# First attention, heads 4 to 7: probabilities turned by VectorE blocks and one exchange through HBM instead of TensorE, with the values one unit later and the branch product behind retention's projections

## The chip, the cores and the metric

The kernel runs on one core of one Trainium2 chip. The metric is device time in microseconds (us). The kernel before took 815.37 us, the median of three runs (815.24 to 815.68). A difference under 0.2% (1.6 us) can't be told from no change.

The engines are named as in the profile: PE (TensorE), DVE (VectorE), ACT (ScalarE), POOL (GpSimd) and SP (SyncE, which here only issues DMAs). Each engine runs its own instructions in order and waits on semaphores that other engines or DMAs raise.

## The reference, cut to what matters

Two layers, each a mixer and a squared-ReLU MLP, on 256 tokens of width 1024. The mixer adds three branches: MLA attention (called the first attention here), MoBA attention, and retention with a group norm.

```python
def causal_attention(q, k, v, scale):            # MLA: 8 heads
    s = einsum('bhqd,bhkd->bhqk', qb, k) * scale  # 128 queries at a time
    p = softmax(where(kpos <= qpos, s, NEG_INF))
    return einsum('bhqk,bhkd->bhqd', p, v)

def hybrid_mixer(h, w_in, ...):
    p = h @ w_in     # all projections: cq, ckv, k_rope, mq, mk, mv, rq, rk, rv, rg, g_mla, g_moba, g_ret
    o_mla, o_moba, o_ret = mla_branch(...), moba_branch(...), retention_branch(...)
    merged = (sigmoid(g_mla) * (o_mla @ w_branch_mla)
              + sigmoid(g_moba) * (o_moba @ w_branch_moba)
              + sigmoid(g_ret) * (o_ret @ w_branch_ret))
    return merged @ w_out
```

With 256 tokens MoBA has a single block, so it is causal attention too. Everything is float32; the kernel keeps that precision by splitting each large operand into a high and a low part and multiplying three times.

## The kernel before, in words

**Units.** The mixer is a list `prog` of units. A unit is a piece of a weight product on PE: in `project` and `branch` one weight block of 128x1024 numbers (512 KB) and 12 matmuls of 512 columns; in `project_turned` one block, 8 matmuls of 512 columns and 8 of 256. `at(slot, job)` hangs other work behind a unit. The order of the units of a layer, before: start or `b0` and `mq`, `mk`, `mv` with `qrope`, `qnope`, `kvup`; the gates `gmla0`, `gmla1`, `gmoba0`, `gmoba1` (4 units each); `bmla0`, `bmla1` (2 each, the first attention's branch product); `rqk` (4 units, retention's queries and keys); `rv`, `rg`, `gret0`, `gret1` (4 each); `bmoba0`, `bmoba1`, `bret0`, `bret1` (2 each); `wout`; then the MLP. Within this order a list scheduler places the instructions of each engine before the program runs, by its own estimate of times. PE's order is fixed by it, and so are DVE's, ACT's and SP's.

**A weight block's way.** SP issues the DMA into a `raw` tile (7 of them), ACT copies it to `whi` (L222), DVE subtracts to `wlo` (L224), PE uses both. `behind` names DMAs after which a weight block is to be issued.

**Attention.** Scores go to four PSUM banks (`ps_s`); DVE adds the mask and takes the maximum, ACT does exp, DVE the reciprocal and the scaling (L538). The values product `po` (L609, L611) needs the probabilities turned, keys along partitions. There are two ways to turn them. `turned_blocks` transposes 32x32 blocks on DVE (a STREAM_TRANSPOSE per head into a tile `blocks`), and `moved_blocks` (L594) moves the blocks to their partitions with 16 DMAs from SBUF to SBUF. `turned` transposes on PE, three 128x128 matmuls against the identity per head into a PSUM bank `ps_pt` (L549), which ACT copies out (L550). The first attention's heads 0 to 3 go the first way, its heads 4 to 7 the second (`homes` = `("probT", None)`), in both layers. MoBA's eight heads go the first way.

**What hangs where.** `first` is the unit at which an attention's scores of heads 0 to 3 start: `mv` 3 for the first attention, `gmoba1` 1 for MoBA. Just ahead of MoBA's first scores stand the first attention's values (`former`). `ret_scores` (`ps_r`) stands behind MoBA's values at `rg` 1. `ret_values` (`por`, L1042 to L1044), `group_norm` and `oret_blocks` hang at `rg` 3.

**Retention's way to its branch.** After `por`: `group_norm` on DVE, POOL and ACT; `oret_blocks` transposes blocks on DVE (L273), one DMA of 512 KB writes them to a `bounce` in HBM (L275) and four of 128 KB read them back turned (`oretturned`, L279); `oret_split` copies them to `oreth` on ACT and to `oretl` on DVE (L264); then PE can start `bret0`. The MLP turns its hidden rows the same way (`hblocks`, `hturned`).

**Rope.** `swapped` (L464) makes the partner halves `qkoth` of queries or keys with four SBUF-to-SBUF DMAs; products with sine and cosine follow (L476). For MoBA in the first layer POOL does them, eight such DMAs for heads 0 to 3 and eight for heads 4 to 7; for retention in both layers DVE does most of it.

Of the kernel before, what the change touches and what calls it, by code (L numbers as in the profile page):

```python
# [7 lines left out]
F32 = mybir.dt.float32  # L8
F32R = mybir.dt.float32r
BF16 = mybir.dt.bfloat16  # L10
AF = mybir.ActivationFunctionType
# [3 lines left out]
P = 128  # L15
D = 1024
S = 256
# [15 lines left out]
QKD = NOPE + ROPE  # L33
# [29 lines left out]
def weight_plan():  # L63

    plan = []

    def block(key, name, kt, cols, per):
        for j in range(0, kt, per):
            plan.append(((*key, j // per), name, (j, per), cols))

    def turned(key, cols):
        for n in range(4):
            block((*key, n), "w_in", KD, cols[P * n : P * n + P], KD)

    def span(c, n):
        return range(c, c + n)

    for l in range(L):
        if l == 0:

            for i in range(2):
                plan.append(((l, "mq", i), "w_in", (0, 1), C_MQ[256 * i : 256 * i + 256]))
            plan.append(((l, "b0", 0), "w_in", (0, 1), C_MLA))
            for k in range(1, KD):
                plan.append(((l, "b0mq", k), "w_in", (k, 1), [*C_MLA, *C_MQ]))
        else:
            block((l, "b0"), "w_in", KD, C_MLA, 2)
            turned((l, "mq"), C_MQ)
        turned((l, "mk"), C_MK)
        block((l, "mv"), "w_in", KD, C_MV, 2)  # L90
        mv, plan = plan[-4:], plan[:-4]
        for i, (key, name, kt, cols) in enumerate(
            (("qrope", "mla_w_q_up", 2, C_QROPE), ("qnope", "mla_w_q_up", 2, C_QNOPE), ("kvup", "mla_w_kv_up", 1, C_KV))
        ):
            block((l, key), name, kt, cols, kt)
            plan.append(mv[i])
        plan.append(mv[3])
        for i in range(2):
            block((l, "gmla%d" % i), "w_in", KD, span(C_GMLA + 512 * i, 512), 2)
        for i in range(2):  # L100
            block((l, "gmoba%d" % i), "w_in", KD, span(C_GMOBA + 512 * i, 512), 2)
        def branch_block(name, i):
            block((l, "b%s%d" % (name, i)), "w_branch_" + name, 4, span(512 * i, 512), 2)

        for i in range(2):
            branch_block("mla", i)
        turned((l, "rqk"), C_RQK)
        block((l, "rv"), "w_in", KD, C_RV, 2)
        block((l, "rg"), "w_in", KD, span(C_RG, 512), 2)
        for i in range(2):  # L110
            block((l, "gret%d" % i), "w_in", KD, span(C_GRET + 512 * i, 512), 2)
        for name, i in LATE:
            branch_block(name, i)
        for n in range(KD):
            block((l, "wout", n), "w_out", KD, span(P * n, P), KD)
        for kind, i in mlp_order():
            if kind == "up":
                g, j = divmod(i, 4)
                plan.append(((l, "up", g, j), "w_mlp_up", (2 * j, 2), span(512 * g, 512)))
            else:  # L120
                plan.append(((l, "down", i, 0), "w_mlp_down", (i, 1), range(D)))
    at, offset = {}, 0
    for key, name, (j, n), cols in plan:
        at[key] = (offset, n, len(cols))
        offset += P * n * len(cols)
    return plan, at, offset
# [22 lines left out]
def trunk(ctx: ExitStack, tc: tile.TileContext, gx, wts, consts, gfin, gn, xtok, out):  # L149


    nc = tc.nc
# [34 lines left out]
        return loaded.pop(key)  # L187


    behind = {}  # L190

    def have(n):

# [39 lines left out]
    def misc_tile(name="misc"):  # L233
        return ps.tile([P, 512], F32, name=name, tag="misc", bufs=4)
# [260 lines left out]
    def in_a_row(*jobs):  # L495


        with tc.manual_schedule(engines={mybir.EngineType.PE}):
            rest = [job() for job in jobs]
        for job in rest:  # L500
            job()
# [14 lines left out]
    def attention_head(scale):  # L516


        got = {}

        def scores(s_ps):
            p = sb.tile([P, 3 * P], F32, name="prob", bufs=4)
            m = small("smx")
            nc.vector.tensor_tensor_reduce(
                p[:, 0:P], s_ps[:, 0:P], mask[:, P : 2 * P], 1.0, NEG_INF, ALU.add, ALU.max, m[:, 0:1]
            )
            nc.vector.tensor_tensor_reduce(
                p[:, P : 3 * P], s_ps[:, P : 3 * P], mask, 1.0, NEG_INF, ALU.add, ALU.max, m[:, 1:2]
            )
            nc.vector.tensor_scalar(m[:, 2:4], m[:, 0:2], -scale, None, op0=ALU.mult)  # L530
            spans = ((0, P), (P, 3 * P))
            for i, (a, b) in enumerate(spans):
                nc.scalar.activation(
                    p[:, a:b], p[:, a:b], AF.Exp, bias=m[:, 2 + i : 3 + i], scale=scale, accum_out=m[:, 4 + i : 5 + i]
                )
            nc.vector.reciprocal(m[:, 6:8], m[:, 4:6])
            for i, (a, b) in enumerate(spans):
                nc.vector.tensor_scalar(p[:, a:b], p[:, a:b], m[:, 6 + i : 7 + i], None, op0=ALU.mult)  # L538
            got["p"] = p

        def turn_blocks(dst):

            return nc.vector.transpose(dst, got["p"])

        def turn(dst):

            pt = misc_tile("ps_pt")
            for i, src in enumerate((0, P, 2 * P)):
                nc.tensor.transpose(pt[:, P * i : P * i + P], got["p"][:, src : src + P], ident)  # L549
            return lambda: nc.scalar.activation(dst, pt[:, : 3 * P], AF.Copy)  # L550

        return scores, turn_blocks, turn

    def attention(oT, vs, scale, first, group, former, gap, turn, homes):

# [5 lines left out]
        def four_tile(h):  # L561
            if h // 4 not in tiles:
                tiles[h // 4] = sb.tile([P, 4 * 3 * P], F32, name="probT", bufs=2)
            return tiles[h // 4]
# [12 lines left out]
                tc.keep_in_program_order(turning)  # L577
            pT[h] = o[:, 0:2], o[:, 2]

        def turned(h):  # L580

            o = four_tile(h)[:, 3 * P * (h % 4) : 3 * P * (h % 4) + 3 * P]
            pT[h] = o[:, 0:S], o[:, S : 3 * P]
            return heads[h][2](o)

        def moved_blocks(h0):


            e = 3 * P
            for a in range(4):  # L590
                for b in range(4):
                    src = pT["blocks"][32 * a : 32 * a + 32, e * b : e * b + e]
                    queue = nc.scalar if h0 and b % 2 else nc.sync
                    dma = queue.dma_start(four_tile(h0)[32 * b : 32 * b + 32, e * a : e * a + e], src)  # L594
                    if former:
                        tc.keep_in_program_order(dma)

# [29 lines left out]
        at(first, lambda: in_a_row(*former, lambda: four(0)))  # L627
        at(first + gap, lambda: in_a_row(lambda: four(4)))
        for i in range(2):
            if homes[i] is None:  # L630
                at(first + turn[i], lambda i=i: in_a_row(*(lambda h=h: turned(h) for h in range(4 * i, 4 * i + 4))))
                continue
            for h in range(4):
                at(first + turn[i] + h // 2, lambda h=4 * i + h: turned_blocks(h, heads[h][1]))
            at(first + turn[i] + 1, lambda i=i: moved_blocks(4 * i))
# [91 lines left out]
    def at(slot, step):  # L727
        steps.setdefault(slot, []).append(step)

    def slot(key, j):  # L730
        return [k for k, _ in prog].index((key, j))
# [8 lines left out]

    def layer(l, xn, before):

        c0 = []
        c, mla, mqkv, rqkv = {}, {}, {}, {}

# [218 lines left out]
        def mla_scores(h0):  # L964
# [4 lines left out]
            return banks  # L969

        mla_last = attention(
            omlaT, lambda: mla["v"], QKD**-0.5, first, mla_scores, (), MLA_GAP, MLA_TURN, ("probT", None)
        )


# [3 lines left out]
        def load_dec():  # L979

            rqkv["dec"] = sb.tile([P, K_TURNED_MB - K_DEC], F32, name="dec", tag="Q", bufs=1)
            tc.keep_in_program_order(nc.sync.dma_start(rqkv["dec"], consts[:, K_DEC:K_TURNED_MB]))

        at(slot("gmoba1", 3), load_dec)
        merged, mT = {}, []
        branch(l, "bmla", range(2), omlaT, th_mla, merged)
        if l == 0:

            for i, (key, j) in enumerate((("gmoba0", 0), ("gmoba0", 1), ("gmoba1", 0), ("gmoba1", 1))):
                at(slot(key, j), lambda i=i: moba_rope(("mk", "mq")[i % 2], i // 2))  # L990
        first = slot("gmoba1", 1)
        at(first, lambda: omobaT.extend((t4("omobah"), t4("omobal"))))

        def moba_scores(h0):
# [87 lines left out]
                split_turned(oret_T[0], oretT)  # L1082

        project_turned(l, "rqk", xn, ret_pair)
        project(l, "rv", xn, 512, ret_done("rv"))


# [38 lines left out]
        branches = {"moba": (omobaT, th_moba), "ret": (oretT, th_ret)}  # L1126
        for name, half in LATE:
            branch(l, "b" + name, [half], *branches[name], merged, between if name == "ret" else None)
        at(slot("rg", 1), lambda: in_a_row(*moba_last, ret_scores))
        for h in range(RT_H):  # L1130
            at(slot("rg", 3), lambda h=h: ret_values(h))
        at(slot("rg", 3), group_norm)
        at(slot("rg", 3), oret_blocks)
        at(slot("bmoba1", 1), oret_split)


# [238 lines left out]
MLA_GAP = 7  # L1375
# [84 lines left out]
```

## Time and profile before

| | |
|---|---|
| median of three runs | 815.37 us |
| the profiled execution's own time | 816.03 us |
| its span, first to last instruction | 814.1 us |
| PE busy in the span | 807.1 us, 99% |
| DVE busy | 577.3 us, 71% |
| ACT busy | 459.9 us, 56% |
| POOL busy | 98.2 us, 12% |
| granted TensorE clock | 0.999 |
| first attention's values on PE in the first layer start at | 100.8 us |
| retention's branch product in the first layer starts at | 196.0 us |

Times in the views are microseconds from the span's start. Matmuls overlap: one of 512 columns is shown as lasting 0.39 us, while the next one starts 0.23 us after it. What PE spends on a matmul is therefore read from start to start.

### The profile page before, as it was taken

To read this page: it belongs to the slowest core of one execution; us is meant where nothing else is said; L and a number is where in the kernel's file an instruction comes from. 1 tells how busy PE (TensorE), PEld (TensorE's weight loads), DVE (VectorE), ACT (ScalarE), POOL (GpSimd) and SP (SyncE) were. 2 spreads that over 40 slices of the span, in tenths; PEclk is the share of its full clock that TensorE was granted. 3 is DMA by queue.
4 is the path that set the end of the run, shared out by engine and by line. 5 is a ranking of instruction groups with operands and counts; after the bars stand their busy time and mean duration, and the time that the engine had idled before them with its cause. 6 is when DMAs were issued, how large, how long until landed. Compare 5 with 4: busy or idle time off the path is not lost.

```text
span 814.1 us, 11424 instructions
## 1 busy us (share of the span) xinstructions
PE 807.1 (99%) x3991; PEld 677.1 (83%) x3991; DVE 577.3 (71%) x950; ACT 459.9 (56%) x722; POOL 98.2 (12%) x75
## 2 busy tenths in 40 slices
PE   9999999999999999999999999999999999999996
PEld 7888888888888888888899888888888888888885
DVE  6879599798786455555598985886898754665554
ACT  7676655445555455555586565645546645555551
POOL 0100440330030000000035221012201200000000
PEclk9999999999999999999999999999999999999999
DMA  9964665767476777776657539448674676898731
GB/s 334 350 232 133 223 219 190 254 217 271 143 224 214 236 256 259 260 256 236 212 176 218 180 107 367 143 130 282 219 239 162 219 242 227 294 301 282 255 133 52
DMA packets 65528, 182.14 MB, mean 224 GB/s; under 512 B 9024, under 2 KB 23744, under 8 KB 65216
## 3 DMA queue, kind: packets, MB, share of 16 engines
q1 hardware_dynamic: 64128, 179.97, 65.8%
q10 hardware_dynamic: 1344, 1.46, 0.6%
q8 instruction: 31, 0.51, 0.3%
q14 instruction: 25, 0.20, 0.1%
HBM read 161.47 MB, written 11.53 MB: 213 GB/s over the span
## 4 chain that ended last, share of the span: by engine, by line
PE 99%; DVE 0%; ACT 0%; issue 0%; DVEq 0%
PE acc L245 18%; PE acc L243 18%; PE acc L244 18%; PE pup L244 7%; PE pup L243 7%; PE pup L245 7%; PE acc L1150 6%; PE acc L442 5%; PE acc L444 2%; PE ps_s L968 1%; PE acc L810 1%; PE po L609 1%; PE ps_s L511 1%; PE warm L721 0%; PE acc L812 0%; PE po L611 0%
## 5 line engine op out<-in xcount | busy, mean ns | idle before, releaser
L224 DVE TENSOR_TENSOR wlo<-raw,whi 128x1024 fp32r<-128x1024 f32 (+4 forms) x287 | 340.6, 1206 | 107.1 <-ACT whi L222 104.7
L222 ACT ACTIVATE whi<-raw 128x1024 fp32r<-128x1024 f32 (+4 forms) x287 | 287.7, 1022 | 167.7 <-PE acc L245 89.6
L243 PE MATMUL acc<-whi,xs 128*128 128x512 f32 (+1 forms) x304 | 118.5, 391 | 0.0
L245 PE MATMUL acc<-whi,xs 128*128 128x512 f32 (+1 forms) x304 | 118.4, 389 | 0.0
L244 PE MATMUL acc<-wlo,xs 128*128 128x512 f32 (+1 forms) x304 | 117.8, 387 | 0.0
L244 PE MATMUL pup<-wlo,xs 128*128 128x512 f32 x256 | 99.8, 390 | 0.0
L243 PE MATMUL acc<-whi,sq 128*128 128x512 f32 x256 | 99.8, 390 | 0.0
L245 PE MATMUL pup<-whi,xs 128*128 128x512 f32 x256 | 99.6, 389 | 0.0
L245 PE MATMUL acc<-whi,sq 128*128 128x512 f32 x256 | 99.6, 389 | 0.0
L244 PE MATMUL acc<-wlo,sq 128*128 128x512 f32 x256 | 99.6, 389 | 0.0
L243 PE MATMUL pup<-whi,xs 128*128 128x512 f32 x256 | 99.3, 389 | 0.0
L264 DVE TENSOR_TENSOR sq<-hturned,sq 128x1024 fp32r<-128x1024 f32 x16 | 19.6, 1225 | 75.5 <-ACT sq L264 75.5
L243 PEld LDWEIGHTS acc<-whi,xs 128*128 128x128 f32 x304 | 57.0, 188 | 11.5 <-issue 0.7
L245 PEld LDWEIGHTS acc<-whi,xs 128*128 128x128 f32 x304 | 57.1, 188 | 11.4
L244 PEld LDWEIGHTS acc<-wlo,xs 128*128 128x128 f32 x304 | 57.1, 188 | 11.0
L264 ACT ACTIVATE sq<-hturned 128x1024 fp32r<-128x1024 f32 x16 | 17.0, 1060 | 79.6 <-DMA hturned<-bounce 79.6
L243 PEld LDWEIGHTS acc<-whi,sq 128*128 128x128 f32 x256 | 48.1, 188 | 10.0
L245 PEld LDWEIGHTS acc<-whi,sq 128*128 128x128 f32 x256 | 48.1, 188 | 10.0
L244 PEld LDWEIGHTS acc<-wlo,sq 128*128 128x128 f32 x256 | 48.0, 188 | 9.9
L245 PEld LDWEIGHTS pup<-whi,xs 128*128 128x128 f32 x256 | 48.1, 188 | 9.8
L244 PEld LDWEIGHTS pup<-wlo,xs 128*128 128x128 f32 x256 | 48.1, 188 | 9.7
L243 PEld LDWEIGHTS pup<-whi,xs 128*128 128x128 f32 x256 | 47.9, 188 | 9.8
(216 smaller groups left out, 1137.5 us busy)
## 6 DMA issues: line engine op xcount, KB each, us to landing
raw<-wts SPq DMA_DIRECT2D x264, 512.0 KB, 4.6
bounce<-hblocks SPq DMA_DIRECT2D x16, 512.0 KB, 4.7
hturned<-bounce SPq DMA_DIRECT2D x64, 128.0 KB, 2.9
probT<-blocks SPq DMA_DIRECT2D x80, 48.0 KB, 2.0
qkoth<-qkraw SPq DMA_DIRECT2D x48, 64.0 KB, 2.4
raw<-wts SPq DMA_DIRECT2D x5, 464.0 KB, 6.0
dec<-consts SPq DMA_DIRECT2D x2, 1024.0 KB, 6.6
raw<-wts SPq DMA_DIRECT2D x4, 416.0 KB, 4.1
```

The source lines that it names most:

```text
L222: fetched.append(nc.scalar.activation(hi[:, cs], raw[:, cs], AF.Copy))
L224: nc.vector.tensor_sub(lo[:, cs], raw[:, cs], hi[:, cs].bitcast(F32))
L243: nc.tensor.matmul(o, ah, bh, start=start, stop=False, **more)
L244: nc.tensor.matmul(o, ah, bl, start=False, stop=False, **more)
L245: nc.tensor.matmul(o, al, bh, start=False, stop=stop, **more)
L264: return nc.scalar.activation(hi, src, AF.Copy), nc.vector.tensor_sub(lo, src, hi.bitcast(F32))
L442: nc.tensor.matmul(acc, wh[:, k, :], xn.both(k), start=k == 0, stop=False)
L444: nc.tensor.matmul(acc[:, 0:S], wl[:, k, :], xn.k(k)[0], start=False, stop=k == KD - 1)
L511: mm = nc.tensor.matmul(bank[:, o], a[rows, sa], b[rows, sb_], start=True, stop=True)
L609: nc.tensor.matmul(dst, vh, pT[h + j][0], start=True, stop=False)
L810: nc.tensor.matmul(mq[n], wq[n][0], xn.both(k), start=k == 0, stop=False)
L1150: nc.tensor.matmul(o, a, b, start=half == 0 and i == 0, stop=4 * half + n == KD and i == len(jobs) - 1)
```

## The change

The first attention's heads 4 to 7 are turned by DVE blocks as well, into the tile of the keys (`"KK"`, whose readers are done by then). The PE way and its ACT copies are gone from the program. For these four heads `moved_blocks` no longer issues 16 DMAs from SBUF to SBUF: one DMA of 768 KB writes the blocks to `pbounce` in HBM, and four of 192 KB read them back into `probT`, one for each band of 32 partitions.

SP would otherwise be free to issue other DMAs between; `behind` and `issue_after` set two of them after the exchange: the load of retention's decay table `dec` (1 MB), and one weight block (the first layer's fourth `rqk` block, the second layer's second `bmla0` block).

The units are reordered. `rqk` comes right behind `gmoba1`, and `bmla0` and `bmla1` come behind `rqk`. The first attention's values and MoBA's first scores move from `gmoba1` 1 to `gmoba1` 2. MoBA's values and `ret_scores` move from `rg` 1 to `rg` 2, and `ret_values`, `group_norm` and `oret_blocks` from `rg` 3 to `gret0` 0. `oret_split` stays at `bmoba1` 1.

```diff
@@ weight_plan
+        turned((l, "rqk"), C_RQK)
         for i in range(2):
             branch_block("mla", i)
-        turned((l, "rqk"), C_RQK)
@@ attention_head, attention
-        def turn(dst):
-            pt = misc_tile("ps_pt")
-            for i, src in enumerate((0, P, 2 * P)):
-                nc.tensor.transpose(pt[:, P * i : P * i + P], got["p"][:, src : src + P], ident)
-            return lambda: nc.scalar.activation(dst, pt[:, : 3 * P], AF.Copy)
...
         def moved_blocks(h0):
             e = 3 * P
+            tile_ = four_tile(h0)
+            if h0 and not former:
+                bounce = dr.tile([P, 4 * e], F32, name="pbounce", bufs=1)
+                nc.sync.dma_start(bounce, pT["blocks"])
+                for b in range(4):
+                    src = bounce.rearrange("(a p) (b r) -> b p a r", a=4, b=4)[b]
+                    dst = tile_[32 * b : 32 * b + 32].rearrange("p (a r) -> p a r", a=4)
+                    behind[tuple(mla_next)] = [nc.sync.dma_start(dst, src)]
+                return
             for a in range(4):
                 for b in range(4):
...
         for i in range(2):
-            if homes[i] is None:
-                at(first + turn[i], lambda i=i: in_a_row(*(lambda h=h: turned(h) for h in range(4 * i, 4 * i + 4))))
-                continue
             for h in range(4):
                 at(first + turn[i] + h // 2, lambda h=4 * i + h: turned_blocks(h, heads[h][1]))
             at(first + turn[i] + 1, lambda i=i: moved_blocks(4 * i))
@@ layer
+        mla_next[:] = (l, "bmla0", 1) if l else (l, "rqk", 3, 0)
...
-            omlaT, lambda: mla["v"], QKD**-0.5, first, mla_scores, (), MLA_GAP, MLA_TURN, ("probT", None)
+            omlaT, lambda: mla["v"], QKD**-0.5, first, mla_scores, (), MLA_GAP, MLA_TURN, ("probT", "KK")
...
-            tc.keep_in_program_order(nc.sync.dma_start(rqkv["dec"], consts[:, K_DEC:K_TURNED_MB]))
-        at(slot("gmoba1", 3), load_dec)
+            with tc.issue_after(behind[tuple(mla_next)][0].ins):
+                tc.keep_in_program_order(nc.sync.dma_start(rqkv["dec"], consts[:, K_DEC:K_TURNED_MB]))
-        branch(l, "bmla", range(2), omlaT, th_mla, merged)
-        first = slot("gmoba1", 1)
+        first = slot("gmoba1", 2)
...
         project_turned(l, "rqk", xn, ret_pair)
+        branch(l, "bmla", range(2), omlaT, th_mla, merged)
+        at(slot("rqk", 0), load_dec)
...
-        at(slot("rg", 1), lambda: in_a_row(*moba_last, ret_scores))
+        at(slot("rg", 2), lambda: in_a_row(*moba_last, ret_scores))
         for h in range(RT_H):
-            at(slot("rg", 3), lambda h=h: ret_values(h))
-        at(slot("rg", 3), group_norm)
-        at(slot("rg", 3), oret_blocks)
+            at(slot("gret0", 0), lambda h=h: ret_values(h))
+        at(slot("gret0", 0), group_norm)
+        at(slot("gret0", 0), oret_blocks)
         at(slot("bmoba1", 1), oret_split)
```

What the scheduler makes of it is shown at three places. In its rows `x2` or `x12` is a count of equal instructions in a row.

The first place is PE at the first attention's end in the first layer, before. The twelve transposes stand in `gmla1`/`gmoba0` work (`acc<-whi,xs`), and 36 matmuls later all of the values product, heads 0 to 3 and 4 to 7, in one piece:

```order
L245 MATMUL acc<-whi,xs_91 128x512
L549 MATMUL ps_pt<-K,prob 128x128 x12
L243 MATMUL acc<-whi,xs_92 128x512
...
L245 MATMUL acc<-whi,xs_90 128x512
L609 MATMUL po<-probT,vml 64x256 x2
L611 MATMUL po<-probT,vml 64x128 x2
```

The same place with the change; the two halves of `po` are apart by four matmuls of `gmoba1`, and MoBA's scores follow the second:

```order
L245 MATMUL acc<-whi,xs_91 128x512
L605 MATMUL po<-probT,vml 64x256 x2
L607 MATMUL po<-probT,vml 64x128 x2
L605 MATMUL po<-probT,vml 64x256 x2
L607 MATMUL po<-probT,vml 64x128 x2
L243 MATMUL acc<-whi,xs_92 128x512
L244 MATMUL acc<-wlo,xs_92 128x512
L245 MATMUL acc<-whi,xs_92 128x512
L243 MATMUL acc<-whi,xs_92 128x512
L605 MATMUL po<-probT,vml 64x256 x2
L607 MATMUL po<-probT,vml 64x128 x2
```

The transposes are gone, `po` starts 12 matmuls of 512 columns later in the row of the others, and in the first layer it is in two pieces; in the second layer it stays in one.

The second place is SP in the first layer, from the exchange of heads 0 to 3 to that of MoBA's. Before:

```order
L594 DMA probT<-blocks 32x384 x16
L464 DMA qkoth<-qkraw 32x512 x8
L207 DMA raw<-wts 128x1024
L982 DMA dec<-consts 128x2048
L207 DMA raw<-wts 128x1024 x6
L464 DMA qkoth<-qkraw 32x512 x8
L207 DMA raw<-wts 128x1024 x11
L594 DMA probT<-blocks 32x384 x16
```

With the change:

```order
L590 DMA probT<-blocks 32x384 x16
L464 DMA qkoth<-qkraw 32x512 x8
L580 DMA pbounce<-blocks 128x1536
L207 DMA raw<-wts 128x1024 x3
L464 DMA qkoth<-qkraw 32x512
L584 DMA probT<-pbounce 32x4x384 x4
L464 DMA qkoth<-qkraw 32x512 x7
L977 DMA dec<-consts 128x2048
L207 DMA raw<-wts 128x1024 x12
```

The exchange's write takes the place behind the first eight `qkoth` copies; three weight blocks go ahead of its reads, and seven of the second eight `qkoth` copies, `dec` and the other weight blocks stand behind the reads.

The third place is DVE in retention's group norm, first layer (the second is alike). Before:

```order
L1056 TENSOR_SCALAR gve<-gmv 128x4 x2
L224 TENSOR_TENSOR wlo<-raw,whi 128x1024
L1068 TENSOR_SCALAR oret<-por,gmv,gve 128x128 x4
L1062 SCALAR_TENSOR_TENSOR goff<-gmv,gve 128x4
L1072 SCALAR_TENSOR_TENSOR oret<-oret,half,rg 128x512
L224 TENSOR_TENSOR wlo<-raw,whi 128x1024
```

With the change:

```order
L1049 TENSOR_SCALAR gve<-gmv 128x4 x2
L224 TENSOR_TENSOR wlo<-raw,whi 128x1024
L1061 TENSOR_SCALAR oret<-por,gmv,gve 128x128 x4
L224 TENSOR_TENSOR wlo<-raw,whi 128x1024
L1055 SCALAR_TENSOR_TENSOR goff<-gmv,gve 128x4
L1065 SCALAR_TENSOR_TENSOR oret<-oret,half,rg 128x512
L224 TENSOR_TENSOR wlo<-raw,whi 128x1024
```

One more weight subtraction stands inside the norm. On PE, 124 matmuls stood between the last `por` and the first of `bret0` in both layers; now 114 in the first layer and 113 in the second.

More of the change, by code (lines that the diff above doesn't have):

```diff
@@ L187, in load_w @@
         return loaded.pop(key)
-    behind = {}
+    behind, mla_next = {}, []
     def have(n):
@@ L543, in turn_blocks @@
             return nc.vector.transpose(dst, got["p"])
-        def turn(dst):
-            pt = misc_tile("ps_pt")
-            for i, src in enumerate((0, P, 2 * P)):
-                nc.tensor.transpose(pt[:, P * i : P * i + P], got["p"][:, src : src + P], ident)
-            return lambda: nc.scalar.activation(dst, pt[:, : 3 * P], AF.Copy)
-        return scores, turn_blocks, turn
+        return scores, turn_blocks
     def attention(oT, vs, scale, first, group, former, gap, turn, homes):
@@ L578, in turned_blocks @@
             pT[h] = o[:, 0:2], o[:, 2]
[L580 to L584, printed above, removed]
         def moved_blocks(h0):
             e = 3 * P
+            tile_ = four_tile(h0)
[7 more added lines that the diff above has]
+                return
             for a in range(4):
@@ L593, in moved_blocks @@
                     queue = nc.scalar if h0 and b % 2 else nc.sync
-                    dma = queue.dma_start(four_tile(h0)[32 * b : 32 * b + 32, e * a : e * a + e], src)
+                    dma = queue.dma_start(tile_[32 * b : 32 * b + 32, e * a : e * a + e], src)
                     if former:
```

## The prediction

> **What bounds the kernel now.** I read the page's busy times and its chain of waits first, then PE's waits, then the timeline of each engine at the places that the change touches.
>
> ```profile
> PE 807.1 (99%) x3991; PEld 677.1 (83%) x3991; DVE 577.3 (71%) x950; ACT 459.9 (56%) x722; POOL 98.2 (12%) x75
> PE 99%; DVE 0%; ACT 0%; issue 0%; DVEq 0%
> PE warm L721 <- PEq L1453: 0.8, 1, 0.8
> L549 PE MATMUL ps_pt<-K,prob x24: 270/272/273, 91.2 to 494.6; 128*128 128x128 f32 x24
> ```
>
> PE is busy all the time, the chain that ended last is PE's own stream, and PE's only wait is 0.8 us at the start. So the kernel ends when PE has gone through its list. Time taken from DVE, ACT or SP is worth nothing; a matmul taken out of PE's list is worth its distance to the next start; any new wait of PE is lost in full. The 24 transposes stand in that list.
>
> **Term 1, the transposes.** PE's timeline, first layer (start, duration, operation, count):
>
> ```profile
> 90.53 0.39 PE L243 MATMUL acc<-whi,xs 128*128 128x512 f32 x1
> ...
> 90.98 0.40 PE L245 MATMUL acc<-whi,xs 128*128 128x512 f32 x1
> 91.22 1.47 PE L549 MATMUL ps_pt<-K,prob 128*128 128x128 f32 x12
> 92.45 0.48 PE L243 MATMUL acc<-whi,xs 128*128 128x512 f32 x1
> 92.77 0.39 PE L244 MATMUL acc<-wlo,xs 128*128 128x512 f32 x1
> 100.50 0.39 PE L245 MATMUL acc<-whi,xs 128*128 128x512 f32 x1
> 100.81 0.65 PE L609 MATMUL po<-probT,vml 128*64 128x256 f32 x4
> ```
>
> Two steps from 90.53 to 90.98 give 0.225 us from one 512-column matmul to the next. Without the transposes the start at 92.77 would come two steps after 90.98, at 91.43: 1.34 us less. The second layer has the same twelve, with the same durations in the tile's view above: together −2.68. The ACT copies that go too were on no path of PE.
>
> The Trainium skill, "VectorE: DVE Perf Modes", sections "The three transpose paths" and "Rules for kernel authors", speaks against the change: it gives about 390 ns for TensorE's 128x128 transpose and 311 for VectorE's, and advises TensorE where a PSUM result will do. By 390 ns the removal would be worth 24 x 0.39 = 9.4 us, an estimate from that page; the rows put the twelve in 1.23 us, 0.10 each, and the measurement decides.
>
> **Term 2, `po` in two pieces.** Entering and leaving such a piece costs a little: 100.50 to 100.81 is 0.31 against 0.225, and 92.45 to 92.77 is 0.32. Together +0.18 for the additional interruption in the first layer; none in the second.
>
> **Term 3, retention's norm, which starts later and must end earlier.** Two moves meet: `por` goes down by a unit, and `bret0` comes 10 (first layer) and 11 matmuls nearer to it. At 0.225 that is 2.25 and 2.5 us less time. The path, in rows picked from the timelines of PE, DVE, SP and ACT:
>
> ```profile
> 167.67 0.39 PE L1044 MATMUL por<-rv,retA 128*128 128x128 f32 x2
> 168.33 0.88 DVE L1054 BATCH_NORM_STATS2 gst<-por 128x6 f32<-128x128 f32 x4
> 178.57 1.22 DVE L224 TENSOR_TENSOR wlo<-raw,whi 128x1024 fp32r<-128x1024 f32 x1
> 179.71 0.70 DVE L273 STREAM_TRANSPOSE oretblocks<-oret 128x512 f32<-128x512 f32 x1
> 180.44 0.33 SPq L275 DMA_DIRECT2D bounce<-oretblocks  x1
> 187.11 1.75 SPq L279 DMA_DIRECT2D oretturned<-bounce  x4
> 192.14 1.06 ACT L264 ACTIVATE oreth<-oretturned 128x1024 fp32r<-128x1024 f32 x1 [0.30 <-DMA oretturned<-bounce]
> 193.83 1.22 DVE L264 TENSOR_TENSOR oretl<-oretturned,oreth 128x1024 fp32r<-128x1024 f32 x1
> 196.92 0.62 PE L245 MATMUL acc<-whi,oretl 128*128 128x512 f32 x2
> 583.58 0.33 SPq L275 DMA_DIRECT2D bounce<-oretblocks  x1
> 594.81 1.07 ACT L264 ACTIVATE oreth<-oretturned 128x1024 fp32r<-128x1024 f32 x1 [0.74 <-DMA oretturned<-bounce]
> ```
>
> From `por`'s end (168.06) to PE's need of `oretl` (196.92) there were 28.86 us; now 26.6. The path takes 0.27 to the first BATCH_NORM, 12.08 from there to the end of the block transposes (180.41), 11.7 from the bounce's issue at 180.44 to the copy on ACT, 1.06 for the copy, 1.22 for `oretl`: 26.35. DVE's list has one more `wlo` inside the norm, and 178.57 to 179.71 prices it at 1.14: 27.5, so 0.9 late. In the second layer the exchange is 11.23 (583.58 to 594.81), the rest taken as alike, and 26.4 are there: 27.0, 0.6 to 0.7 late. What 11.7 will be is open. The MLP's exchange is of the same size (KB of one DMA, median us from issue to landing):
>
> ```profile
> bounce<-hblocks SPq DMA_DIRECT2D x16, 512.0 KB, 4.7
> hturned<-bounce SPq DMA_DIRECT2D x64, 128.0 KB, 2.9
> raw<-wts SPq DMA_DIRECT2D x264, 512.0 KB, 4.6
> ```
>
> At 4.7 + 2.9, with 1.3 for three of four reads' issues (187.11, 1.75), it would be 8.9 and nothing would be late. As an upper bound I put half that distance, 1.4, on top in each layer. I take 0.9 + 0.7 = +1.6, since these rows are of retention's own exchange; bounds 0 and +4.4. All of PE's stream stands behind these waits.
>
> **Term 4, a PSUM bank.** `rqk` now precedes `bmla0`, whose `acc` takes the bank of `rqk`'s first unit once DVE has added it to `qkraw`. That addition stands in DVE's list behind the softmax of MoBA's heads 0 to 3. Between the first of their scores and `bmla0` PE has 16 score matmuls, 8 of 512 columns and four `rqk` units of 8 wide and 8 narrow ones:
>
> ```profile
> 103.57 1.58 PE L511 MATMUL ps_s<-qkT 64*128 64x128 f32 x16
> 130.66 1.10 PE L444 MATMUL acc<-xs,wlo 128*128 128x256 f32 x8
> 131.60 2.00 PE L442 MATMUL acc<-xs,whi 128*128 128x512 f32 x8
> ```
>
> Eight narrow ones take 0.94 (130.66 to 131.60), eight wide ones 8 x 0.225 = 1.8. So PE needs 1.6 + 1.8 + 4 x 2.74 = 14.4 us. DVE started 1.35 after the first score (103.57 to 104.92, next fence), so it has 13.0. What it needs there:
>
> ```profile
> 78.55 0.29 DVE L524 CUSTOM_DVE_ANT_0 prob<-ps_s,K 128x128 f32<-128x128 f32 x1 [0.48 <-PE ps_s L968]
> 85.16 0.55 DVE L538 TENSOR_SCALAR prob<-prob,smx 128x128 f32<-128x128 f32 x2
> 104.92 0.28 DVE L524 CUSTOM_DVE_ANT_0 prob<-ps_s,K 128x128 f32<-128x128 f32 x1
> 109.72 2.72 DVE L538 TENSOR_SCALAR prob<-prob,smx 128x128 f32<-128x128 f32 x2
> 116.60 0.56 DVE L538 TENSOR_SCALAR prob<-prob,smx 128x128 f32<-128x128 f32 x2
> 107.24 1.29 POOL L476 TENSOR_TENSOR qkoth<-qkoth,tab 128x512 f32<-128x512 f32 x1 [8.34 <-ACT prob L533]
> 95.35 11.19 SPq L464 DMA_DIRECT2D qkoth<-qkraw  x8
> L543 DVE STREAM_TRANSPOSE blocks<-prob x24: 534/562/579, 71.0 to 542.6; 128x384 f32<-128x384 f32 x24
> ```
>
> The first two rows are the ends of a softmax of four heads of the first attention, the next three of MoBA's, then POOL, SP and the tile of blocks (ns). Undisturbed, a softmax of four heads is 78.55 to 85.71, less the `wlo` inside it: 6.0. Beside POOL's products it is 104.92 to 117.07, or 12.15: a pair of scalings takes 2.72 beside POOL instead of 0.56 without. In both cases four `wlo` (4.56), two block transposes (1.1) and the addition (0.3, an estimate from the quarter-width rows' 0.28) come on top: 12.0, no wait, or 18.1, 5.1 late. POOL's six products of 1.29 start when the second `qkoth` copies are in (the row names an exp of ACT as its releaser, but the copies were under way until then). These were issued over 11.19 us behind `dec` and seven weight blocks, and now stand behind the exchange and three blocks. By term 5 the first four are issued at 100 to 102.5 and in 2 to 2.5 later, so POOL works from 102 to 105 until 110 to 112.7. The softmax starts at 107.1 and its scalings come in its second half: something under half of the 6.1 of disturbance is left, up to 2.7, which makes 14.7, and by the earlier end of POOL 13 and no wait. I take +0.5, bounds 0 and +5.1.
>
> **Term 5, the first exchange.** DVE's four block transposes (0.56 each) go mostly into its gap of 1.35 ahead of 87.06; the `wlo` behind it come 0.9 later, which no PE wait there has shown:
>
> ```profile
> 87.06 2.36 DVE L224 TENSOR_TENSOR wlo<-raw,whi 128x1024 fp32r<-128x1024 f32 x2 [1.35 <-ACT whi L222]
> 84.80 6.37 SPq L464 DMA_DIRECT2D qkoth<-qkraw  x8
> 91.27 0.53 SPq L207 DMA_DIRECT2D raw<-wts  x1
> ```
>
> SP is through the eight copies at 91.27 and issues the write there. It lands after 4.7 us, or 7.05 for half as many bytes again, at 96 to 98.3; the reads are issued then over 1.75, and a copy takes SP 0.8 (6.37 / 8). Retention's reads took 5.0 (187.11 to 192.14) for 512 KB, 7.5 scaled: landed at 101 to 105.8. PE comes to the second half of `po` at 100.81 − 1.34 + 12 x 0.225 + 1.38 (half of 100.81 to 103.57) + 4 x 0.225 = 104.4; MoBA's scores follow at 105.8, DVE at 107.1. I take 0, bounds 0 and +1.4. In the second layer the same sum leaves over 1 us to spare. SP waits for the write before it can issue a read, and seven copies, `dec` and weight blocks queue behind; the fourth `rqk` block is issued at about 106, in and split by 114, and used from 105.8 + 1.6 + 1.8 + 8.2 = 117.4: 3 us of cover.
>
> The Trainium skill, "DMA: Bandwidth & Descriptors", section "Anatomy of one DMA — SWDGE (gpsimd) path", warns that a write's completion can be surprisingly slow when its target is HBM. The MLP's row of 4.7 for such a write, against 4.6 for a weight block's read, shows no such delay; it would act as rival D.
>
> **Sum:** −2.68 + 0.18 + 1.6 + 0.5 + 0 = −0.4. Against the profiled execution, 816.03 (814.1 of span, 1.9 around it), this is 815.6; the median shown is 0.66 below that execution: **815.0**. The likeliest case's own range is 813.8 to 817.0: its waits from 0.9 (one layer's `bret0`) to 4.1 (2.8 at both, 1.3 at the bank) on top of 812.9, the sum without any.
>
> **The rivals.**
>
> A, the forecast (0.50): the gain of the transposes is eaten by small waits at `bret0`, perhaps at `bmla0`.
>
> B, the full gain (0.30). Retention's exchange keeps to the MLP's 4.7 + 2.9 and POOL is early: no new wait, −2.5, **812.9**. For it: the reads at 187.11 went out 6.7 us after their write and SP is idle between. Against: both of retention's exchanges took over 11 us, and more DMAs now lie near.
>
> C, slower (0.15): POOL's products cover MoBA's softmax in the first layer as fully as before, and PE waits 5.1 for the bank ahead of `bmla0` instead of 0.5: **819.6**. It decides from a second set of `qkoth` copies that lands after about 107, when all of POOL's 7.7 us lie in the softmax. For it: that is what the rows 107.24 and 109.72 show. Against: four weight blocks and `dec`, 3 MB, no longer stand ahead of the copies.
>
> D, slower (0.05): the exchange of heads 4 to 7 is late, with a write half as slow again as the bound (10) and 7.5 for the reads, landed at 108.7: 4.3 of wait at the second `po`, **819.2**; from a landing after 104.4. For it: SP's rows show the write behind a full queue of copies. Against: both medians.
>
> That the removal is worth nothing is excluded by PE's chain.
>
> **The numbers.** The range, 812.5 to 817.6, holds B less the spread of the runs shown (0.4), and A up to a bank wait of 2.7 instead of 0.5 (817.2) with the same spread; it leaves out C and D. The bound of 0.2% is 1.6 us, about what can be told from no change: faster means under 813.7, which is B; slower over 817.0, C, D: faster 0.30, same 0.50, slower 0.20.
>
> **What would show it.** No `ps_pt` rows on PE; 32 block transposes of probabilities; PE waits of 0.4 to 1.1 us for `oreth` on ACT or `oretl` on DVE at each `bret0`; a wait below 2 us on DVE's `qkraw` near 120 us; none on `probT`. Wrong: none of these waits (B), one of 4 to 5 us near 120 (C) or 104 (D).

## The result

The changed kernel took 825.09 us, the median of four runs (821.78 to 827.51). The kernel before took 815.49 beside it. The ratio is 1.0115, with a 95% interval of 1.008 to 1.0151: 1.15% slower, some 9.6 us. The forecast was 815.0, with a range of 812.5 to 817.6. One execution among those reported below, of 2,099 us, was slow and is left out of its kernel's ratio.

The transposes are gone, and so is PE's unbroken stream. The first rows are the page's busy times and the chain that ended last, after the change; the others are PE's waits (us in total, times, longest).

```profile
PE 808.9 (98%) x3967; PEld 675.8 (82%) x3967; DVE 566.7 (69%) x958; ACT 454.0 (55%) x714; POOL 90.6 (11%) x75
PE 85%; DMA 5%; DVE 4%; SPq 3%; issue 2%; ACT 1%; DVEq 0%; ACTq 0%
PE acc L243 <- DVE rg L1088: 4.4, 2, 3.6
PE po L605 <- ACT rv L1006: 2.2, 1, 2.2
PE acc L243 <- DVE qkraw L424: 0.6, 1, 0.6
PE acc L243 <- ACT oreth L264: 0.2, 1, 0.2
```

The chain was 99% PE before. Now 15% of it runs through DMAs, DVE, SP's and ACT's issues and ACT; PE mostly works meanwhile, so that this is not a share of lost time. PE has 7.4 us of new waits, and 6.6 of them stand at two places that the forecast does not speak of: the values of MoBA (`po` from `mv`), and the PSUM bank of the gate `rg`, which DVE frees late (L1088).

PE is also shown as busy for longer than before, though it does less. The windows of PE show why (length, busy time, matmuls, granted clock, DMA share, GB/s):

```profile
156.00:158.00 2.00, 0.12 (x2) 1.00 0.64 156
158.00:160.00 2.00, 2.00 (x18) 0.66 0.85 274
160.00:162.00 2.00, 2.00 (x16) 0.50 1.11 375
570.00:572.00 2.00, 1.50 (x6) 0.91 0.96 334
572.00:574.00 2.00, 2.00 (x7) 0.50 1.00 399
574.00:576.00 2.00, 2.00 (x8) 0.73 0.86 350
```

After the waits of 2.2 and 3.6 us the granted clock falls to half for some 3.5 us. In the first layer that loses 2 x (0.34 + 0.50) = 1.7 us, in the second 2 x (0.09 + 0.50 + 0.27) = 1.7.

**The account of the profiled execution.** By the forecast's own rows, the span without any new wait is 814.1 − 2.68 + 0.18 = 811.6. With 7.4 of waits and 3.4 of lost clock that is 822.4, and the span measured is 823.1. I can't place the last 0.7.

**Where the waits come from.** First MoBA's second half (heads 4 to 7) in the first layer before the change, in rows picked from the timelines: its scores on PE, its block transposes on DVE, ACT's and SP's eight DMAs of its exchange, what SP issued ahead of them, ACT's next instruction behind its issues, and its values on PE.

```profile
127.18 1.58 PE L511 MATMUL ps_s<-qkT 64*128 64x128 f32 x16
141.59 1.96 DVE L543 STREAM_TRANSPOSE blocks<-prob 128x384 f32<-128x384 f32 x4 [0.35 <-issue]
140.20 4.96 SPq L464 DMA_DIRECT2D qkoth<-qkraw  x8
143.58 5.15 ACTq L594 DMA_DIRECT2D probT<-blocks  x8
145.28 5.01 SPq L594 DMA_DIRECT2D probT<-blocks  x8
148.83 1.27 ACT L1013 ACTIVATE rv<-acc,ms 128x512 f32<-128x512 f32 x2 [7.36 <-DMA probT<-blocks]
156.05 0.65 PE L609 MATMUL po<-probT,mv 128*64 128x256 f32 x4
```

The same after the change; the last row is from SP's own waits between 140 and 160 us (in total, times, longest):

```profile
129.65 1.58 PE L511 MATMUL ps_s<-qkT 64*128 64x128 f32 x16
130.54 0.69 DVE L479 TENSOR_TENSOR qkT<-qkT,qkoth 128x512 f32<-128x512 f32 x1 [3.24 <-POOL qkoth L476]
145.99 1.95 DVE L543 STREAM_TRANSPOSE blocks<-prob 128x384 f32<-128x384 f32 x4
144.42 2.01 SPq L207 DMA_DIRECT2D raw<-wts  x4
147.97 8.74 SPq L590 DMA_DIRECT2D probT<-blocks  x8
147.97 9.06 ACTq L590 DMA_DIRECT2D probT<-blocks  x8
157.14 1.26 ACT L1006 ACTIVATE rv<-acc,ms 128x512 f32<-128x512 f32 x2 [10.48 <-DMA probT<-blocks]
157.88 0.65 PE L605 MATMUL po<-probT,mv 128*64 128x256 f32 x4 [2.18 <-ACT rv L1006]
159.38 4.63 DVE L224 TENSOR_TENSOR wlo<-raw,whi 128x1024 fp32r<-128x1024 f32 x4 [9.20 <-ACT whi L222]
164.66 0.50 PE L243 MATMUL acc<-whi,xs 128*128 128x512 f32 x1 [0.77 <-DVE rg L1088]
570.50 0.50 PE L243 MATMUL acc<-whi,xs 128*128 128x512 f32 x1 [3.59 <-DVE rg L1088]
SPq L590 <- DMA raw<-wts: 2.0, 1, 2.0
```

Read it in four steps. (1) `rqk` now comes earlier, and its rope with it. DVE idles 3.24 us for POOL's product of that rope, ahead of MoBA's second softmax; the block transposes end 4.4 us later than before (147.94 against 143.55), though the scores are only 2.5 later. (2) What SP issued ahead of the exchange was eight `qkoth` copies of 64 KB; now it is four weight blocks, 2 MB. The eight DMAs of each queue take 8.7 and 9.1 us to issue instead of 5.0 and 5.2; for 2.0 us of that SP waits until a weight block lands before it issues the next copy. (3) PE comes to MoBA's values at 155.7, 0.35 earlier than before, and waits 2.18. The row names ACT's `rv` as the releaser, which stands in ACT's list behind its eight issues. (4) ACT issues half of these DMAs itself. It computes nothing for 10.48 us, 7.36 before, and copies no weight block; DVE, which subtracts from these copies, idles 9.20, then has four `wlo` in a row ahead of the gate's `rg` at L1088. PE waits for the bank that this frees. In the second layer the same delay shows only there, with 3.59.

The Trainium skill, "DMA: Bandwidth & Descriptors", section "Issuing engines are not separate DMA queues", says that DMAs of all engines end up on the same 16 DMA engines and interleave there, whichever engine starts them. ACT's eight copies agree. Behind the weight blocks that SP issued, the slowest of them landed 6.3 us after its issue; with these blocks out of the way (the experiment "The weight blocks held" below) the slowest took 2.2. The change's eight on ACT, in us from issue to landing:

```profile
DMA to landing us min/median/max: 1.9/2.0/6.3
```

### The profile page after: what moved, and what is told of

It reads as the page before. It is cut to its first block, busy times and chain, and to the rows that moved or that the text cites. A ratio compares the mean times of both kernels' runs of the same rounds, so it can differ in the third digit from the quotient of the medians.

```text
span 823.1 us, 11372 instructions
## 1 busy us (share of the span) xinstructions
PE 808.9 (98%) x3967; PEld 675.8 (82%) x3967; DVE 566.7 (69%) x958; ACT 454.0 (55%) x714; POOL 90.6 (11%) x75
## 4 chain that ended last, share of the span: by engine, by line
PE 85%; DMA 5%; DVE 4%; SPq 3%; issue 2%; ACT 1%; DVEq 0%; ACTq 0%
PE acc L243 15%; PE acc L244 14%; PE acc L245 14%; PE pup L243 7%; PE pup L244 7%; PE pup L245 7%; PE acc L1145 5%; PE acc L442 4%; DMA probT<-blocks 2%; SPq L590 2%; PE acc L444 2%; DVE wlo L224 2%; PE ps_s L962 1%; PE acc L804 1%; DMA oretturned<-bounce 1%
```

## The experiments

Two pairs of theories were tested. A: the order of the units costs the time; B: the exchange through HBM does. And within A: A1, the four weight blocks ahead of MoBA's second exchange; A2, DVE's wait for the rope ahead of MoBA's second softmax.

### The order alone

The order of the change, with the PE way of turning put back.

```diff
-            omlaT, ..., MLA_GAP, MLA_TURN, ("probT", "KK")
+            omlaT, ..., MLA_GAP, MLA_TURN, ("probT", None)
-            with tc.issue_after(behind[tuple(mla_next)][0].ins):
-                tc.keep_in_program_order(nc.sync.dma_start(rqkv["dec"], ...))
+            tc.keep_in_program_order(nc.sync.dma_start(rqkv["dec"], ...))
```

with `turn` and `turned` as before the change.

> The units in the order of the change, with heads 4 to 7 of the first attention still turned on PE (the twelve transposes per layer are back, no exchange through HBM). Theory A (the order of the units is what costs: retention's rope now stands ahead of MoBA's second softmax, and four weight blocks stand ahead of MoBA's second exchange): the waits of PE at MoBA's values and at the gate's bank stay, 2 to 4 us in each layer with the lower clock behind them, and the time is 823 to 828 (the change's 825 plus up to 2.7 for the transposes). Theory B (the exchange through HBM and the DMAs that it pushes back are what costs): those waits go, 815 to 817.

Measured: 829.04 us, ratio 1.0169 (1.0154 to 1.0184). PE's waits:

```profile
PE acc L243 <- DVE rg L1103: 7.2, 2, 3.6
PE po L618 <- ACT rv L1021: 3.2, 1, 3.2
```

The same two places, and more of it: 10.4 us. Theory A holds. The order costs 13.4 us by itself, and in that order the exchange is worth about −4, more than its transposes. The time lies 1 us above the upper end of what was expected.

### The exchange alone

The change with all reordering undone: `bmla` ahead of `rqk`, MoBA's `first` at `gmoba1` 1, its values at `rg` 1, `ret_values`, `group_norm` and `oret_blocks` at `rg` 3, `load_dec` at `gmoba1` 3. The block that is set behind the exchange is the one in the same place of the list.

```diff
-        mla_next[:] = (l, "bmla0", 1) if l else (l, "rqk", 3, 0)
+        mla_next[:] = (l, "rqk", 1, 0) if l else (l, "bmla1", 1)
-        first = slot("gmoba1", 2)
+        first = slot("gmoba1", 1)
```

> The exchange through HBM for heads 4 to 7 of the first attention, with the order of the units as before the change. Theory A (order): no wait of PE at MoBA's values, since retention's rope comes after MoBA's second softmax again; the second half of the first attention's values may wait 0 to 3 us for its exchange in a layer: 813 to 817. Theory B (exchange): waits at MoBA's values of 2 to 4 us in each layer, 820 to 826.

Measured: 815.60, ratio 1.0003 (0.9993 to 1.0012). No wait at MoBA's values or the gate's bank: theory B falls. Beside 0.6 for `omlal`, what eats the gain of the transposes is a wait in the second layer for the new exchange itself. PE's wait; SP's timeline of that place; two windows of PE, around that wait and behind it:

```profile
PE po L605 <- DMA probT<-pbounce: 2.1, 1, 2.1
485.31 3.16 SPq L207 DMA_DIRECT2D raw<-wts  x6
489.53 0.33 SPq L580 DMA_DIRECT2D pbounce<-blocks  x1
498.42 1.81 SPq L584 DMA_DIRECT2D probT<-pbounce  x4
502.00:504.00 2.00, 0.52 (x8) 1.00 1.03 263
506.00:508.00 2.00, 2.00 (x20) 1.00 1.01 408
```

Six weight blocks, 3 MB, go ahead of the write, and its reads can be issued only 8.9 us after it. This wait, 2.05 us in one piece, is followed by a full clock.

### The weight blocks held

```diff
                     if former:
                         tc.keep_in_program_order(dma)
+                    if former and h0 and queue is nc.sync:
+                        for key in (("gret0", 2), ("gret0", 3), ("gret1", 0), ("gret1", 1)):
+                            behind[mla_next[0], *key] = [dma]
```

> The change, with the four weight blocks that SP issues between MoBA's two exchanges (gret0's third and fourth, gret1's first and second) held until the second exchange's DMAs are issued. Theory A1 (these 2 MB ahead of the sixteen small DMAs make the exchange late and keep ACT busy issuing): the sixteen land 1.9 to 2.1 us after their issue, ACT needs 5.2 us for its eight instead of 9.1, no wait at MoBA's values and none at the gate's bank, 813.5 to 817. Theory A2 (MoBA's second softmax comes too late already, through DVE's wait of 3 to 4 us for POOL's product of retention's rope): half of the waits stay, 818 to 822.

Measured: 815.68, ratio 1.0003 (0.9994 to 1.0013). This one edit takes back all of the loss, 9.4 us. SP's and ACT's issues, and what is left of PE's waits beside 0.8 and 0.3 at the start:

```profile
133.00 19.53 SPq L590 DMA_DIRECT2D probT<-blocks  x24
147.57 5.29 ACTq L590 DMA_DIRECT2D probT<-blocks  x8
PE po L608 <- DMA probT<-pbounce: 0.4, 1, 0.4
PE acc L243 <- DVE qkraw L424: 0.3, 1, 0.3
```

ACT's eight take 5.29 us again, though they begin at 147.57, as late as in the change. So A1 holds: that MoBA's second half is late is borne, the 2 MB ahead of its exchange are not.

### The rope's addition on POOL

```diff
-    def rope_turned(raw, tab, engine, late=False):
+    def rope_turned(raw, tab, engine, late=False, add=None):
-        engine.tensor_add(o, o, other)
+        (add or engine).tensor_add(o, o, other)
-            rT.append(rope_turned(raw, rqkv["tab"], nc.vector))
+            rT.append(rope_turned(raw, rqkv["tab"], nc.vector, add=nc.gpsimd))
```

> The change, with the last addition of retention's rope (qkT with qkoth, two per layer) on POOL instead of DVE, so that DVE doesn't wait for POOL's product ahead of MoBA's second softmax. SP's order is the same. Theory A2 (DVE's wait is what makes MoBA's second half late): its block transposes come 3 to 4 us earlier, the waits at MoBA's values and at the gate's bank go, 813.5 to 817. Theory A1 (the weight blocks in the queue): the exchange still takes 9 us from ACT's first issue to its last, waits of 1 to 3 us in each layer stay, 818 to 823.

Measured: 819.35, ratio 1.0046 (1.0031 to 1.0061).

```profile
143.71 1.96 DVE L543 STREAM_TRANSPOSE blocks<-prob 128x384 f32<-128x384 f32 x4 [1.06 <-DMA probT<-blocks]
145.70 9.29 ACTq L590 DMA_DIRECT2D probT<-blocks  x8
PE acc L243 <- DVE rg L1088: 3.0, 2, 2.5
PE po L605 <- ACT rv L1006: 0.4, 1, 0.4
```

The transposes come 2.3 us earlier, ACT's issuing still takes 9.29, and waits of 3.4 stay. A1's expectation is met, A2's is not; but A2's share is real, 5.7 us of the 9.4: a delay of 2.3 decides over how much of the exchange's lateness reaches PE.

### Both, and the second layer's exchange first

Three kernels: the last two edits together; the held blocks with the second layer's new exchange ahead of three weight blocks; all three edits.

```diff
-        mla_next[:] = (l, "bmla0", 1) if l else (l, "rqk", 3, 0)
+        mla_next[:] = (l, "rqk", 1, 0) if l else (l, "rqk", 3, 0)
```

> Both edits at once: the four weight blocks held behind MoBA's second exchange, and the last addition of retention's rope on POOL. If the two delays add up in one chain (rope, then MoBA's softmax, then blocks, then exchange), either cure leaves slack and the second adds little: 813.5 to 815.5, with no wait of PE over 0.5 us at MoBA's values or at the gate's bank. If holding the blocks was a chance of the schedule and POOL's additional products get in DVE's way, it is slower than the held blocks alone: 816 to 819.

> The held blocks, and in the second layer the exchange of the first attention's heads 4 to 7 ahead of three weight blocks that SP issued before it (the order of DMAs is set behind the exchange from rqk's second block on, instead of from bmla0's second). If transfers are served in the order of issue, the write lands some 3.5 us earlier, the wait of 0.4 us at the second half of the values in the second layer goes, and the kernel gains 0.4 to 1 us on the held blocks alone: 814 to 815.5. If not, no change, 815 to 816.5; if the three blocks come too late for PE, slower, 817 or more.

> The change with all three edits: blocks held, rope's addition on POOL, second layer's exchange first. If the edits are independent: 813 to 814.5. If POOL's products cost DVE time: 815 to 818.

Measured: 815.44 for the two edits, ratio 0.9997 (0.9988 to 1.0006); that its waits are under 0.5, as expected, no trace of it shows. 817.28 for the second, ratio 1.0025 (1.0015 to 1.0034). 815.87 for all three, ratio 1.0006 (0.9997 to 1.0015).

The first is as expected of one chain with two cures: the second adds nothing that can be measured. The other two did not gain what was hoped for: 817.28 lies in the range given for blocks that come too late, 815.87 in the one given for POOL's products costing DVE time, and no run shows that POOL is the reason. PE's largest waits in the second kernel:

```profile
PE acc L243 <- ACT oreth L264: 1.0, 1, 1.0
PE acc L243 <- DVE qkraw L424: 0.7, 1, 0.7
PE acc L442 <- ACT th L641: 0.7, 1, 0.7
```

The wait for `pbounce` is gone as meant, 0.4. A new one of 0.7 came in the second layer, at `rqk`, for a bank that ACT frees; all three edits show it too, with 0.7. In the second kernel's trace ACT idles 4.23 and 3.86 us for weight blocks shortly before, at 499 to 508 us, which it does not with the held blocks alone. That ACT is late because the three blocks now come later is therefore likely; it was not tested. The waits at `oreth` and `qkraw` are in the first layer, whose code this edit does not touch, so much of the 1.6 us between this kernel and the held blocks alone stays open.

### The exchange alone, ahead of the blocks

```diff
-        mla_next[:] = (l, "rqk", 1, 0) if l else (l, "bmla1", 1)
+        mla_next[:] = (l, "bmla0", 0) if l else (l, "bmla1", 1)
```

> The exchange in the order of the units from before the change, and in the second layer four weight blocks that SP issued ahead of it now behind it. If these 2 MB are what made PE wait 2.05 us for the exchange in the second layer, the wait goes and what is left is the gain of the transposes less 0.6 at the branch's bank: 813 to 814.2. If the exchange is late for another reason, 815 to 816.5.

Measured: 813.85, ratio 0.9979 (0.9971 to 0.9988). PE's only new wait, and SP in the second layer:

```profile
PE acc L245 <- DVE omlal L264: 0.7, 1, 0.7
484.81 1.00 SPq L207 DMA_DIRECT2D raw<-wts  x2
489.31 0.33 SPq L580 DMA_DIRECT2D pbounce<-blocks  x1
492.59 1.75 SPq L584 DMA_DIRECT2D probT<-pbounce  x4
```

The reads go out 3.3 us after the write instead of 8.9, and the wait of 2.05 is gone. This is the expected effect of the order in the queue, in the order of the units from before.

In the first layer one more block behind the exchange:

```diff
-        mla_next[:] = (l, "bmla0", 0) if l else (l, "bmla1", 1)
+        mla_next[:] = (l, "bmla0", 0) if l else (l, "bmla1", 0)
```

> The exchange in the order from before the change with the second layer's exchange first (the kernel at 813.85), and in the first layer one more weight block issued behind the exchange, by which the second half of the values stands 11 matmuls earlier on PE. If the wait of 0.7 for omlal at the branch product comes from the late second half: it goes, and the time is 813 to 813.5. If the exchange is then late: a wait of 0.5 to 2 us on the reads, 814 to 816.

Measured: 813.46, ratio 0.9973 (0.9962 to 0.9983). The wait for `omlal` is gone; one of 0.3 for ACT's `th` stands in the second layer. This is the fastest kernel of the study, 0.27% under the one before the change; between it and 813.85 the runs do not decide.

### The transposes in the held order

The kernel with the order alone, and the edit that holds the four blocks.

> The order of the units of the change with the four weight blocks held behind MoBA's second exchange, and heads 4 to 7 of the first attention turned on PE as before the change. Against the held blocks with the exchange (815.7) it says what the transposes are worth where nothing else waits. If they are worth their distance on PE, 1.3 per layer, and the exchange costs nothing: 818 to 818.6. If the waits come back with the transposes, as the order alone was 3.9 slower than the change: 819 to 822. If the exchange costs PE as much as it saves: 815.5 to 816.5.

Measured: 818.62, ratio 1.0033 (1.0021 to 1.0046). Against the held blocks with the exchange (815.68) that is 2.9 us more. It is within 0.1 of the first expectation, though its trace has 1.9 us of waits beside the one at the start (1.3 of them for `rg` in the first layer) and that of the held blocks 1.0, so that the transposes themselves are not read more closely than that.

### MoBA's second exchange on SP alone

```diff
-                    queue = nc.scalar if h0 and b % 2 else nc.sync
+                    queue = nc.sync
```

> The change, with all sixteen DMAs of MoBA's second exchange issued by SP, none by ACT. If PE's wait at the gate's bank comes from ACT, which is held in issuing while its copies of weight blocks wait: this wait (3.6 in the second layer, 0.8 in the first) goes; the sixteen are issued later, 0.63 each behind each other, so that the wait at MoBA's values is 3 to 6 us longer in both layers: 824 to 832. If the wait at the bank has another source (a late transfer alone), both waits grow: 830 to 838.

Measured: 822.89, ratio 1.0088 (1.0074 to 1.0102). PE's waits at MoBA's values, one per layer, and the window behind the first:

```profile
PE po L605 <- issue: 4.6, 1, 4.6
PE po L605 <- DMA probT<-blocks: 1.2, 1, 1.2
162.00:164.00 2.00, 2.00 (x14) 0.60 0.93 348
```

No wait for `rg` is left in either layer. So the wait at the bank came through ACT's issuing, as step (4) above says. The wait at the values grew by 2.4 in the first layer and to 1.2 in the second, less than expected, and the time lies under the expected range. The median is 2.2 us below the change's, but the intervals of the two ratios overlap: whether freeing ACT gained more than the longer issue cost is not decided.

## Why the prediction was wrong

**What bounds the kernel** was right: every loss is a wait of PE. "Any new wait of PE is lost in full" put the price too low: by the windows above, the waits of 2.2 and 3.6 cost another 1.7 each in clock.

**Term 1** held. With the exchange in the old order and one wait of 0.3, the kernel is 2.06 us faster (1.4 to 3.1 by its interval), where −2.68 + 0.18 + 0.3 = −2.2 follows from the forecast's terms. In the order of the change the pair of held kernels gives 2.9; their traces differ by 0.9 in other waits. The 9.4 us that follow from the 390 ns of the Trainium skill ("VectorE: DVE Perf Modes", section "The three transpose paths") are not there. **Term 2** is inside that difference and not told apart.

**Term 3** had the place and not the size: a wait for `oreth` in the first layer of 0.2 in the change, 0.4 and 1.0 in two experiments, none in the second layer, against 0.9 and 0.7. In the change's first layer the norm took 12.3 us from `por` to the end of the block transposes, where 13.5 were summed, and the exchange 12.6 instead of 11.7.

**Term 4** had the place and, by luck, the size: 0.6 at the bank for DVE's `qkraw`, where 0.5 was forecast. The forecast put it down to scalings that POOL still disturbs. In the trace POOL is done at 113.4, before the scalings begin at 115.3, and four of them take 0.99 us; what delays DVE in this softmax is a late weight block, for whose copy on ACT it idles:

```profile
110.99 1.30 DVE L224 TENSOR_TENSOR wlo<-raw,whi 128x1024 fp32r<-128x1024 f32 x1 [2.26 <-ACT whi L222]
```

Rival C, POOL over the whole softmax, did not come.

**Term 5** held in the first layer. In the second, "over 1 us to spare" held in the trace of the change, which shows no such wait, but not safely: it was summed from a median landing, and six weight blocks stood ahead of the write. PE waited 2.05 in the exchange alone, 1.2 with MoBA's exchange on SP and 0.4 with the blocks held. Rival D named a late exchange, in the other layer.

**The step that failed** is the pricing of the moved `rqk`. Terms 4 and 5 followed it to its PSUM bank and to its fourth weight block. They left out what else it issues: eight `qkoth` copies, two products on POOL and two additions on DVE per layer, and the gap that these leave behind. The copies had stood between MoBA's two exchanges; with the change they went ahead, and four blocks of 512 KB took their place. No term and no rival has MoBA's second exchange in it, and that is where 6.6 of the 7.4 us of waits stand. SP's list with the change has these blocks in it; the prediction reads that list only around the first exchange. With the four blocks held, the time is 815.68, against a forecast of 815.0: the terms that were there sum to about the right number, and the missing one is worth 9.4 us. That the number is so near is partly luck: the trace of that kernel has no wait for `oreth`, which the sum has at 1.6, and its executions lie between 814.53 and 817.25.

## What to carry to other kernels

When a unit moves, follow each DMA that it issued, and ask what the scheduler will put in the place that they leave: here 2 MB of weights that nobody needed soon went ahead of sixteen small DMAs that PE was about to wait for. An engine that issues DMAs beside its work is held as long as its issues are, here 10.48 us on ACT, and everything behind it is late, so look for its next instructions on the path too. Before trusting a cover in a kernel that is bound by PE, add to each possible wait of some 2 us or more the slower clock that can follow it.

## What was not expected of the hardware

A wait of PE can cost more than its length. In four traces (the change, the order alone, the rope's addition on POOL, MoBA's exchange on SP) the granted clock fell to 0.5 around or behind six waits, of 2.2, 2.5, 3.6 (three) and 4.6 us, and stayed low for some 3 to 7 us; 1.7 us were lost at each of the two in the change. It did not fall behind 2.05 us, nor directly behind one of 3.2. The length alone does not decide. The Trainium skill, "TensorE: Matmul & The Clock Gate", section "Part 1: The HAM clock gate (the "warmup" mystery)", tells of a half-rate state set by a free-running window of about 3.4 us; the half rate agrees with the rows. The rule on the same page of the Trainium skill, no idle gaps over about 3.4 us (section "HAM oscillation — how this bites in real kernels"), does not keep a kernel safe here: 2.2 was enough.

The wide spread of the changed kernel, 821.78 to 827.51 against 815.24 to 815.68 before, goes with these waits. The clock alone does not make it: the execution of 825.30 us has a mean granted clock of 0.998, that of 821.78 one of 0.996. What else does stays open.
